# A two-layer hybrid trunk on one core: the attention heads' steps set further apart, and three output products taken together

## The chip, the cores and the metric

The kernel runs on one core of a Trainium2 chip. The metric is the time of one execution on the device in microseconds (us). All times are of one core; the profile shows one execution, taken by the hardware profiler.

The engines are called PE (TensorE, matrix products), ACT (ScalarE), DVE (VectorE), POOL (GpSimd) and SP (SyncE, which here issues the DMAs).

## The reference

A residual stream of 256 tokens by 2048 passes through two layers. In the first, the mixer is forgetting attention (FoX, 16 heads of 128); in the second, it is a dilated sliding-window attention (8 heads with values of 256; three groups of scores each). Every mixer stands behind an RMS norm and is followed by an RMS norm and a squared-ReLU MLP with 8192 hidden units. Everything is in 32-bit floating point.

```
def fox_attention(h, w_in, b_f, q_gain, k_gain, w_out):
    proj = h @ w_in
    q, k, v, f = jnp.split(proj, [H * dh, 2 * H * dh, 3 * H * dh], axis=-1)
    q = rms_norm(q.reshape(B, S, H, dh), q_gain)      # per head; k in the same way
    c = jnp.cumsum(jax.nn.log_sigmoid(f + b_f), axis=1)
    s = q @ k^T * dh**-0.5 + c[query] - c[key]         # causal
    o = softmax(s) @ v
    return o @ w_out

def dilated_attention(...):                            # q and k per group g, one shared v
    for g, (window, r) in enumerate(((128, 1), (512, 4), (2048, 16))):
        # causal window of 128 steps of stride r, ALiBi slope per (g, head)
    # the groups' numerators and denominators merged; o @ w_out

def reference(...):
    for i in range(2):
        x = x + mixer_i(rms_norm(x, mix_norm_g[i]))
        x = x + relu(rms_norm(x, mlp_norm_g[i]) @ w_up)**2 @ w_down
```

## The kernel before

**Products in three parts.** A 32-bit matrix product is made of three products of reduced-width operands: high part by high part, high by low, low by high. Each operand is therefore held as a cast high part and a low part, which is what the cast left over. Weights arrive from memory in chunks of 2048 rows by 512 columns, by DMAs of two tiles of 128 rows (`raw`). `split` (from L321) makes two such tiles ready at a time: a cast on ACT (`wh`, L333) and a subtraction on DVE (`wl`, L334). There are five buffers of `wh` and `wl`, so a cast must wait until PE has used up an older pair.

**Steps.** `product_steps` (L356) works through a chunk in 16 *steps*. One step is one 128-row tile of the weights against both halves of the 256 tokens: 6 products of 128 by 512 (L368 to L370). After each step the program calls `jobs.tick()`.

**The order of the work.** Everything that is not a product is a *job*: a Python generator that issues some instructions and then says `yield n`, which means that it goes on after n further steps, or `yield key`, which means that it goes on once the named result has been issued. So the program is interleaved while it is written down, by counting steps. From step 24 on, `pin()` fixes the order on each engine to that in which the instructions were written. No engine can go on with a later instruction when an earlier one waits. A wait behind `behind(...)` only puts an instruction behind another in that order.

**The jobs in the attention layers.** In FoX, the columns are worked in four groups `j` of four heads: a chunk of queries, one of keys, one of values. In the dilated layer, there are four groups `q4` of two heads.

* `qk_chain` (L543) norms a chunk of queries or keys: squares on ACT (`sq`), their sums on DVE (`ss`, L553 and L554), a power on POOL (L556), scaling on DVE (`rq`, `qn`, L560 and L562), a transpose of 32 by 32 blocks on DVE (L571), eight block moves to memory and two back over SP, and at last the casts on ACT (L595) and subtractions on DVE (L597).
* `fox_head` (L760) loads the bias, adds the mask (L773), and lets PE form the scores (`sc_f`, L687 and L690). DVE adds the bias and takes the maximum (`nm_f`, L789), ACT takes the exponential (L792), DVE scales by the denominator (L797).
* `p_turned` (L634) transposes the probabilities by way of memory: 32 by 32 blocks on DVE (L638), four block moves, one move back. `p_split` (L648) makes the high part on ACT (`pTh`, L653) and the low part on DVE (`pTl`, L655). Then `pv` (L618) forms the product with the values (`po_f`, `po_d`; L627 and L628) and splits its result into high (`oTfh`, L630) and low part (`oTfl`, L631), which the output product takes.
* `dil_head` (L810) does the same with three sets of scores (`sc_d`, added to the distances in `sd`, L823), one maximum (`nm_d`, L829) and one exponential (L832) for the three. The last of the eight heads is turned by PE (`p_transposed`, `ptp_d`, L662) and not by way of memory.

**Output products and norms.** `out_proj` (L901) multiplies the heads' results by the output weights, four chunks of 512 columns. `in_pair` (L382) takes the first two chunks together: the first 12 rows of one, the first 12 of the other, then the last 4 of each; so the last heads have 24 steps until their rows are wanted. `add_chain` (L878) adds the result to the residual stream and starts the next norm's transposition (`norm_chain`, L492). The tables of distances for the dilated layer (`dilation_tables`, L209) are made at the beginning of the first MLP.

## Time and profile before

| | |
|---|---|
| median of 3 runs | 2225.78 us (2223.76 to 2228.35) |
| profiled execution, its own time | 2224.2 us |
| its span in the profile | 2222.5 us |
| mean granted clock of PE | 0.99 |
| PE busy | 2161.3 us, 97% |
| weight loads of PE (PEld), beside it | 1915.4 us, 86% |
| DVE busy | 1431.6 us, 64% |
| ACT busy | 1089.2 us, 49% |
| DMA moved | 471.57 MB, 212 GB/s on average |

The span is what lies between the first and the last instruction; the execution's own time is 1.7 us longer. Busy times are sums over the whole span. A row of the wait view says which instruction waited for which, how long in total, how often, and the longest. A row of the window view gives the busy time of each engine in one stretch of time. Names of tiles stand without their numbers where rows are grouped. Lines (L655) are those of the kernel before.

### The profile page before, as it was taken

The page shows a single profiled execution, that of the slowest core. Times are in us where ns is not written, and L with a number is a line of the kernel's source. Part 1 is how long each engine was busy: PE and PEld are TensorE (multiplying, and loading weights), DVE is VectorE, ACT ScalarE, POOL GpSimd, SP SyncE. Part 2 cuts the span into 40 slices and gives each one's busy share as a digit, 9 for nine tenths or more (in the row PEclk, how much of TensorE's full clock was granted, in tenths as well). Part 3 has the DMA queues.
Part 4 walks back from the last instruction along what each step waited for, and adds up shares of the span by engine and source line. Part 5 has one row for each costly group of instructions (what it writes and reads, how often), then busy time and mean ns, then how long its engine had stood idle before and what let it go on. Part 6 is the DMA issues. An engine that isn't in the chain of part 4 may idle for free.

```text
span 2222.5 us, 29937 instructions
## 1 busy us (share of the span) xinstructions
PE 2161.3 (97%) x11123; PEld 1915.4 (86%) x11123; DVE 1431.6 (64%) x1892; ACT 1089.2 (49%) x1522; POOL 53.0 (2%) x40
## 2 busy tenths in 40 slices
PE   9989888999999999999999999999999999999998
PEld 7877777888898898898888888878988988988987
DVE  6666766775565565566667787767665665665664
ACT  5544544654354354355555655545544444444442
POOL 0000000000000000000010000100000000000000
PEclk9999999999999999999999999999999999999999
DMA  7776675766656656656777767757666666666663
GB/s 243 220 231 203 199 233 189 257 201 217 205 184 218 205 184 217 204 185 232 257 223 239 234 205 238 229 191 247 226 209 202 203 203 201 202 203 202 200 213 133
DMA packets 313810, 471.57 MB, mean 212 GB/s; under 512 B 35832, under 2 KB 123328, under 8 KB 313664
## 3 DMA queue, kind: packets, MB, share of 16 engines
q1 hardware_dynamic: 313072, 468.99, 65.8%
q8 instruction: 87, 1.43, 0.3%
q10 hardware_dynamic: 560, 0.66, 0.1%
q14 instruction: 59, 0.48, 0.1%
q0 software_dynamic: 32, 0.02, 0.0%
HBM read 446.15 MB, written 23.42 MB: 211 GB/s over the span
## 4 chain that ended last, share of the span: by engine, by line
PE 75%; DVE 3%; DMA 2%; ACT 2%; issue 1%; SPq 1%; POOL 0%; ACTq 0%; DVEq 0%; POOLq 0%
PE acc L369 15%; PE acc L368 15%; PE acc L370 15%; PE up_n3a_acc L432 5%; PE up_n1a_acc L432 5%; PE up_n3a_tp L432 3%; PE up_n3a_sc L432 3%; PE up_n3a_acc L436 3%; PE up_n1a_tp L432 2%; PE up_n1a_acc L436 2%; PE up_n1a_sc L432 2%; DMA raw<-in_dil_w_in_dram 2%; DVE wl L334 1%; PE up_n3a_tp L436 1%; PE up_n3a_sc L436 1%
## 5 line engine op out<-in xcount | busy, mean ns | idle before, releaser
L334 DVE TENSOR_TENSOR wl<-raw,wh 128x1024 fp32r<-128x1024 f32 (+1 forms) x801 | 968.3, 1220 | 639.5 <-ACT wh L333 632.5
L333 ACT CAST wh<-raw 128x1024 fp32r<-128x1024 f32 (+1 forms) x801 | 828.3, 1045 | 868.2 <-PE acc L370 572.2
L368 PE MATMUL acc<-wh,hT_n 128*128 128x512 f32 x896 | 346.3, 387 | 0.1
L369 PE MATMUL acc<-wl,hT_n 128*128 128x512 f32 x896 | 343.5, 383 | 0.1
L370 PE MATMUL acc<-wh,hT_n 128*128 128x512 f32 x896 | 342.6, 383 | 0.0
L368 PE MATMUL acc<-wh,aTh_n1a 128*128 128x512 f32 x512 | 194.0, 379 | 0.0
L369 PE MATMUL acc<-wl,aTh_n1a 128*128 128x512 f32 x512 | 194.0, 379 | 0.0
L370 PE MATMUL acc<-wh,aTl_n1a 128*128 128x512 f32 x512 | 194.0, 379 | 0.0
L370 PEld LDWEIGHTS acc<-wh,hT_n 128*128 128x128 f32 x896 | 171.5, 191 | 24.9
L368 PEld LDWEIGHTS acc<-wh,hT_n 128*128 128x128 f32 x896 | 172.0, 192 | 23.9 <-ACT wh L333 0.5
L369 PEld LDWEIGHTS acc<-wl,hT_n 128*128 128x128 f32 x896 | 171.8, 192 | 23.4 <-DVE wl L334 0.4
L368 PE MATMUL acc<-wh,aTh_n3a 128*128 128x512 f32 x480 | 181.9, 379 | 0.0
L369 PE MATMUL acc<-wl,aTh_n3a 128*128 128x512 f32 x480 | 181.9, 379 | 0.0
L370 PE MATMUL acc<-wh,aTl_n3a 128*128 128x512 f32 x480 | 181.9, 379 | 0.0
L432 PE MATMUL up_n1a_acc<-hT_n,wh 128*128 128x512 f32 x512 | 181.6, 382 | 0.0
L432 PE MATMUL up_n3a_acc<-hT_n,wh 128*128 128x512 f32 x512 | 181.6, 382 | 0.0
L436 PE MATMUL up_n1a_acc<-hT_n,wl 128*128 128x256 f32 x512 | 139.6, 273 | 0.0
L436 PE MATMUL up_n3a_acc<-hT_n,wl 128*128 128x256 f32 x512 | 139.6, 273 | 0.0
L369 PEld LDWEIGHTS acc<-wl,aTh_n1a 128*128 128x128 f32 x512 | 96.8, 189 | 13.7
L370 PEld LDWEIGHTS acc<-wh,aTl_n1a 128*128 128x128 f32 x512 | 96.8, 189 | 13.7
L368 PEld LDWEIGHTS acc<-wh,aTh_n1a 128*128 128x128 f32 x512 | 96.8, 189 | 13.7
L432 PEld LDWEIGHTS up_n3a_acc<-hT_n,wh 128*128 128x128 f32 x512 | 96.8, 189 | 13.5
(680 smaller groups left out, 3183.6 us busy)
## 6 DMA issues: line engine op xcount, KB each, us to landing
raw<-in_mlp_w_up_dram SPq DMA_DIRECT2D x256, 512.0 KB, 4.4
raw<-in_mlp_w_down_dram SPq DMA_DIRECT2D x256, 512.0 KB, 4.4
raw<-in_dil_w_in_dram SPq DMA_DIRECT2D x192, 256.0 KB, 4.4
raw<-in_fox_w_in_dram SPq DMA_DIRECT2D x95, 512.0 KB, 5.0
raw<-in_fox_w_out_dram SPq DMA_DIRECT2D x32, 512.0 KB, 3.8
raw<-in_dil_w_in_dram SPq DMA_DIRECT2D x32, 512.0 KB, 3.8
raw<-in_dil_w_out_dram SPq DMA_DIRECT2D x32, 512.0 KB, 5.2
blocks_n<-turned_n SPq DMA_DIRECT2D x96, 64.0 KB, 3.6
```

The source lines that it names most:

```text
L333: issued["cast"] = nc.scalar.copy(hi[:, part, :], raw[:, part, :])
L334: issued["cut"] = nc.vector.tensor_sub(lo[:, part, :], raw[:, part, :], hi[:, part, :].bitcast(F32))
L368: nc.tensor.matmul(acc[t], ah[:, tok], hi, start=first, stop=False)
L369: nc.tensor.matmul(acc[t], ah[:, tok], lo, start=False, stop=False)
L370: issued["product"] = nc.tensor.matmul(acc[t], al[:, tok], hi, start=False, stop=last)
L432: issued["product"] = nc.tensor.matmul(banks[b], hi[:, i, col], in_turn(tokens.rearrange("p x s -> p (x s)"), P // 2), start=first, stop=last)
L436: nc.tensor.matmul(banks[b][:, 0:S], lo[:, i, col], in_turn(tokens[:, 0, :], P // 2), start=False, stop=False)
```

## The change

Nothing is computed differently but for the turning of the last dilated head. What changes is the number of steps between the instructions of the jobs, and with it the order on every engine.

* **Scores to values.** In `fox_head` the exponential stands two steps behind the scores and not one, the scaling four and not two, the move back nine and not six, the high cast of the turned probabilities fifteen and not eleven, the low subtraction seventeen (two steps behind its cast and no longer with it), and the values nineteen and not thirteen or fourteen. In the last group (j = 3) the cast stands at fourteen, the subtraction at sixteen and the values at seventeen. The heads start at (3, 9, 21, 27) and, in the last group, (3, 8, 13, 17).
* **Bias.** It is loaded eight steps ahead of the scores, and added two steps ahead of them.
* **Dilated heads.** The three scores stand two steps apart, the exponential two steps behind the last, and the values as in FoX. The second head of a group starts eight steps behind the first. The last head of all is turned by way of memory like the others. Within `pv`, the low part of a head's result is subtracted a step behind the cast.
* **Query and key norms.** The casts on ACT stand three steps earlier, and the subtractions on DVE two steps behind their casts.
* **Output products.** Three chunks and not two are taken together, behind both attention layers; the third has its own banks (`ps_tp`). The norm of the third chunk starts after six steps and not two.
* **Tables and the rest.** `dilation_tables` waits for 40 steps and then issues a piece every four steps. The squares of the norm go to another buffer (`sd`). The low part of the values is subtracted a step later; the gate's `c_q` has two steps instead of one.

```diff
 def out_proj / add_out                       # the plan of loads follows the same order
-        if pair:
-            in_pair(lambda n: sums(), lambda acc, ks: product_steps(acc, keys, lhs, ks), posts)
-        for n in range(2 if pair else 0, NX):
+        if group:
+            in_group(lambda n: sums(*(() if n < 2 else (ps_tp, "tp"))),
+                     lambda acc, ks: product_steps(acc, keys, lhs, ks), posts[0:group])
+        for n in range(group, NX):
...
 def qk_chain
-        yield 7
-        for t in range(NT):
-            yield 2
+        yield 6
+        for t in range(NT):
+            subs = []
...
                 nc.scalar.copy(a, of)
-                with behind(issued["cut"]):
-                    nc.vector.tensor_sub(b, of, a.bitcast(F32))
+                subs.append((b, of, a))
+            yield 2
+            for b, of, a in subs:
+                nc.vector.tensor_sub(b, of, a.bitcast(F32))
...
 def pv
             nc.scalar.copy(hi, by_token(po))
+            yield 1
             nc.vector.tensor_sub(lo, by_token(po), hi.bitcast(F32))
...
 def p_turned / p_split
-        yield 4
+        yield 5
         move(turned.rearrange("p i b r -> p (i b r)"), blocks.rearrange("j c i x -> (j c) (i x)"))
-        yield 5
+        yield landing
...
         with behind(issued["cast"]):
             nc.scalar.copy(hi, first)
+        yield 2
         with behind(issued["cut"]):
             nc.vector.tensor_sub(lo, first, hi.bitcast(F32))
...
 def fox_head
-        at = ((2, 4, 6, 9) if j == 3 else (2, 8, 20, 26))[hh]
+        at = ((3, 8, 13, 17) if j == 3 else (3, 9, 21, 27))[hh]
...
-            yield at - 4
+            yield at - 8
...
-        yield 4
+        yield 6
         nc.vector.tensor_add(bias, bias, tables["mask"])
+        yield 2
...
-        turned = yield from p_turned(s, f"f{h}")
+        turned = yield from p_turned(s, f"f{h}", 5 if j == 3 else 6)
         yield ("fv", j)
-        pt_sb = p_split(turned, f"f{h}")
-        yield 2 if j == 3 else 3
+        pt_sb = yield from p_split(turned, f"f{h}")
+        yield 1 if j == 3 else 2
...
 def dil_head
-        yield (5 if q4 == 3 else 6) * i + 2
+        yield 8 * i + 3
...
-        if (q4, i) == (3, 1):
-            yield 2
-            pt_sb = p_transposed(p, f"d{h}")
-        else:
-            turned = yield from p_turned(p, f"d{h}")
-            yield ("dv", q4)
-            pt_sb = p_split(turned, f"d{h}")
-        yield 3
+        turned = yield from p_turned(p, f"d{h}", 6)
+        yield ("dv", q4)
+        pt_sb = yield from p_split(turned, f"d{h}")
+        yield 2
```

How this moves the instructions shows at three places on DVE. In the rows, the number behind a name is the tile's, `wl` is the low part of two tiles of weights, `ss`, `rq`, `qn` and `sq` belong to the norm of the next chunk of queries or keys, `pTl` is the low part of a head's turned probabilities and `oTfl` that of its result.

*First place: the third head of the first FoX group (`f2`), whose probabilities are finished while the keys of the second group are normed.* Before:

```order
L638 STREAM_TRANSPOSE turned_f3_1373<-s_f3_1343 128x3x4x32
L334 TENSOR_TENSOR wl44_1393<-raw44_1244,wh44_1392 128x1024
L553 TENSOR_REDUCE ss_('fk', 1)_1404<-sq_('fk', 1)_0_1400 128x4
L553 TENSOR_REDUCE ss_('fk', 1)_1404<-sq_('fk', 1)_1_1402 128x4
L554 TENSOR_SCALAR ss_('fk', 1)_1404<-ss_('fk', 1)_1404 128x8
L655 TENSOR_TENSOR pTl_f2_1419<-turned_f2_1291,pTh_f2_1418 128x256
L334 TENSOR_TENSOR wl45_1429<-raw45_1279,wh45_1428 128x1024
```

And of the change:

```order
L642 STREAM_TRANSPOSE turned_f3_1397<-s_f3_1335 128x3x4x32
L554 TENSOR_REDUCE ss_('fk', 1)_1408<-sq_('fk', 1)_0_1404 128x4
L554 TENSOR_REDUCE ss_('fk', 1)_1408<-sq_('fk', 1)_1_1406 128x4
L555 TENSOR_SCALAR ss_('fk', 1)_1408<-ss_('fk', 1)_1408 128x8
L600 TENSOR_TENSOR fqT1_0l_928<-sq_('fq', 1)_0_1144,fqT1_0h_927 128x256
L600 TENSOR_TENSOR fqT1_1l_931<-sq_('fq', 1)_0_1144,fqT1_1h_930 128x256
L335 TENSOR_TENSOR wl45_1433<-raw45_1274,wh45_1432 128x1024
L561 TENSOR_SCALAR rq_('fk', 1)_1412<-rq_('fk', 1)_1412,rstd_n0_111 128x4
L563 TENSOR_TENSOR qn_('fk', 1)_0_1445<-acc32_0_1154,rq_('fk', 1)_1412 128x512
...
L335 TENSOR_TENSOR wl46_1469<-raw46_1298,wh46_1468 128x1024
L335 TENSOR_TENSOR wl47_1491<-raw47_1328,wh47_1490 128x1024
L660 TENSOR_TENSOR pTl_f2_1481<-turned_f2_1303,pTh_f2_1480 128x256
```

The low part of the head's probabilities stood ahead of the norm's scaling, for which POOL has to be waited, and stands behind it now, with three weights between.

*Second place: the last heads of FoX.* Before:

```order
L631 TENSOR_TENSOR oTfl_12_3286<-po_f13_0_3317,oTfh_12_3285 128x256
L655 TENSOR_TENSOR pTl_f14_3325<-turned_f14_3185,pTh_f14_3324 128x256
L334 TENSOR_TENSOR wl110_3335<-raw110_3179,wh110_3334 128x1024
L631 TENSOR_TENSOR oTfl_14_3347<-po_f14_0_3348,oTfh_14_3346 128x256
L334 TENSOR_TENSOR wl111_3362<-raw111_3221,wh111_3361 128x1024
```

And of the change:

```order
L635 TENSOR_TENSOR oTfl_12_3311<-po_f13_0_3384,oTfh_12_3310 128x256
L335 TENSOR_TENSOR wl114_3405<-raw114_3255,wh114_3404 128x1024
L335 TENSOR_TENSOR wl115_3426<-raw115_3299,wh115_3425 128x1024
L660 TENSOR_TENSOR pTl_f14_3411<-turned_f14_3264,pTh_f14_3410 128x256
L335 TENSOR_TENSOR wl116_3453<-raw116_3328,wh116_3452 128x1024
L635 TENSOR_TENSOR oTfl_14_3439<-po_f14_0_3440,oTfh_14_3438 128x256
```

The head's low part stood ahead of the weights 110 and stands behind the weights 115 now.

*Third place: the first head of the second dilated group (`d2`), beside the second head (`d3`) and the norm of the next group.* Before:

```order
L838 TENSOR_TENSOR p_d3_11552<-p_d3_11552,sd3_11481 128x384
L638 STREAM_TRANSPOSE turned_d3_11557<-p_d3_11552 128x3x4x32
L334 TENSOR_TENSOR wl460_11571<-raw460_11415,wh460_11570 128x1024
L553 TENSOR_REDUCE ss_('dqk', 2, 0)_11581<-sq_('dqk', 2, 0)_0_11577 128x4
...
L554 TENSOR_SCALAR ss_('dqk', 2, 0)_11581<-ss_('dqk', 2, 0)_11581 128x8
L334 TENSOR_TENSOR wl461_11602<-raw461_11444,wh461_11601 128x1024
L655 TENSOR_TENSOR pTl_d2_11609<-turned_d2_11461,pTh_d2_11608 128x256
L560 TENSOR_SCALAR rq_('dqk', 2, 0)_11585<-rq_('dqk', 2, 0)_11585,rstd_n2_3885 128x4
```

And of the change:

```order
L824 TENSOR_REDUCE nm_d3_11557<-sd3_11500 128x1 x2
L554 TENSOR_REDUCE ss_('dqk', 2, 0)_11565<-sq_('dqk', 2, 0)_0_11561 128x4
...
L335 TENSOR_TENSOR wl461_11587<-raw461_11434,wh461_11586 128x1024
L561 TENSOR_SCALAR rq_('dqk', 2, 0)_11569<-rq_('dqk', 2, 0)_11569,rstd_n2_3869 128x4
...
L335 TENSOR_TENSOR wl462_11626<-raw462_11463,wh462_11625 128x1024
L830 RECIPROCAL den_d3_11558<-den_d3_11558 128x2
...
L642 STREAM_TRANSPOSE turned_d3_11638<-p_d3_11633 128x3x4x32
L335 TENSOR_TENSOR wl463_11658<-raw463_11484,wh463_11657 128x1024
L335 TENSOR_TENSOR wl464_11682<-raw464_11523,wh464_11681 128x1024
L660 TENSOR_TENSOR pTl_d2_11671<-turned_d2_11493,pTh_d2_11670 128x256
```

Here too the scaling of the norm, and besides it that of the second head, now stand ahead of the first head's low part.

More of the change, by code (lines that the diff above doesn't have):

```diff
@@ L241, in add, with add_group @@
             plan.append((w, r, cols))
-    def add_pair(*chunks):
+    def add_group(*chunks):
         for rows in ((0, CUT * P), (CUT * P, D)):
@@ L249, in add_out @@
     def add_out(w):
-        add_pair(*((w, [(n * NC, NC)]) for n in range(2)))
-        for n in range(2, NX):
+        add_group(*((w, [(n * NC, NC)]) for n in range(3)))
+        for n in range(3, NX):
             add(w, (0, D), [(n * NC, NC)])
@@ L261, in add_mlp @@
             if b == 0:
-                add_pair(*((mlp_w_up[l], [(n * NC, NC)]) for n in range(2)))
+                add_group(*((mlp_w_up[l], [(n * NC, NC)]) for n in range(2)))
             for n in range(0 if b else 2, 4):
@@ L272, in trunk @@
         if q4 == 0:
-            add_pair((dil_w_in[0], value), (dil_w_in[0], heads[0]))
+            add_group((dil_w_in[0], value), (dil_w_in[0], heads[0]))
         for cols in heads[1:] if q4 == 0 else heads + [value]:
@@ L353, in trunk, with sums @@
     used = [0]
-    def sums():
-        return [ps_acc.tile([P, NC], F32, tag="acc", name=f"acc{used[0]}_{t}") for t in range(NT)]
+    def sums(pool=ps_acc, tag="acc"):
+        return [pool.tile([P, NC], F32, tag=tag, name=f"acc{used[0]}_{t}") for t in range(NT)]
     def product_steps(acc, keys, lhs, steps):
@@ L380, in product, with in_group @@
         jobs.spawn(post(acc))
-    def in_pair(new, steps, posts):
+    def in_group(new, steps, posts):
         banks = []
-        for n in range(2):
+        for n in range(len(posts)):
             banks.append(new(n))
             steps(banks[n], range(CUT))
-        for n in range(2):
+        for n in range(len(posts)):
             steps(banks[n], range(CUT, KC))
@@ L656, in p_split @@
         return p_hi, p_lo, turned[:, :, 2, :]
-    def p_transposed(p, name):
-        pt = ps_tp.tile([P, 3 * P], F32, tag="tp", name=f"ptp_{name}")
-        for b in range(3):
-            nc.tensor.transpose(pt[:, b * P:(b + 1) * P], p[:, b * P:(b + 1) * P], ident)
-        p_hi, p_lo = (work.tile([P, S], F32R, tag=f"pT{x}", name=f"pT{x}_{name}", bufs=2) for x in "hl")
-        p_whole = work.tile([P, P], F32, tag="s", name=f"pTw_{name}", bufs=S_BUFS)
-        nc.scalar.copy(p_hi, pt[:, 0:S])
-        nc.vector.tensor_sub(p_lo, pt[:, 0:S], p_hi.bitcast(F32))
-        nc.scalar.copy(p_whole, pt[:, S:3 * P])
-        return p_hi, p_lo, p_whole
     def heads_pair(name, slot, keys):
@@ L953, in mlp @@
             if b == 0:
-                in_pair(lambda n: up_banks(key, n), steps, posts)
+                in_group(lambda n: up_banks(key, n), steps, posts[0:2])
             for n in range(0 if b else 2, 4):
```

44 lines of the change are left out of this document (23 added, 21 removed).

## The prediction

> **What bounds the kernel now.** I read the page first, then busy time by stage, then who keeps TensorE (PE) waiting.
>
> ```profile
> PE 2161.3 (97%) x11123; PEld 1915.4 (86%) x11123; DVE 1431.6 (64%) x1892; ACT 1089.2 (49%) x1522; POOL 53.0 (2%) x40
> ```
>
> PE is the bound: what can be gained is its idle time and its slow time. The windows below are the FoX layer with its projections, the first MLP, the dilated layer, the second MLP, and 50 us of undisturbed products (columns: window, length, busy time and instructions of PE, PEld, DVE, ACT, POOL, granted clock, DMA share, GB/s).
>
> ```profile
> 12.00:362.00 350.00, 311.41 (x1466) 267.36 (x1466) 242.38 (x432) 180.52 (x311) 17.41 (x11) 0.95 0.71 219
> 362.00:1205.00 843.00, 842.05 (x4403) 751.81 (x4402) 538.06 (x651) 413.80 (x550) 11.75 (x6) 1.00 0.67 216
> 1205.00:1485.00 280.00, 269.16 (x1301) 234.08 (x1300) 210.47 (x308) 155.39 (x231) 20.57 (x8) 0.98 0.70 223
> 1800.00:1850.00 50.00, 50.00 (x233) 43.80 (x232) 30.04 (x32) 22.29 (x26) 0.00 (x0) 1.00 0.61 203
> ```
>
> The last row gives the unit of time: 50.00/233 = 0.2146 us a product, six to a step (one 128-row of a weight chunk), so **1.29 us a step**. PE's idle time is 350.00−311.41 = 38.6 in FoX, 0.95 in the MLP and 10.8 in the dilated layer: **50.4 us**. Its causes:
>
> ```profile
> PE po_f L627 <- ACT pTh_f L653: 18.7, 5, 4.8
> PE po_f L627 <- DVE pTl_f L655: 14.0, 9, 2.3
> PE sc_d L687 <- DVE sd L823: 7.2, 8, 3.2
> PE sc_f L690 <- ACT fkT_0h L595: 3.4, 4, 1.5
> PE ptp_d L662 <- DVE p_d L840: 3.2, 1, 3.2
> PE sc_f L690 <- DVE fkT_0l L597: 1.4, 4, 0.4
> PE up_n1a_tp L436 <- DVE wl L334: 0.9, 1, 0.9
> ...
> ACT s_f L792 <- DVE nm_f L789: 78.1, 16, 9.5
> DVE bias L773 <- DMA bias<-negc: 33.5, 7, 6.4
> ACT wh L333 <- PE acc L370: 572.2, 369, 7.2
> ```
>
> (What waits, for what: total, times, longest.) Two thirds, 18.7+14.0, is the value product (po_f) standing for its turned probabilities (pTh, pTl). Behind that stand DVE, held up to 6.4 us by the bias landing, and ACT, held up to 9.5 by DVE's maximum: every engine runs its recorded order, so one late instruction holds the weights behind it. The last row sets the pace: ACT's weight casts wait for PE to give buffers back, so ACT and DVE cannot work ahead.
>
> A second loss is the clock. Seven stretches of half clock in the body sum to 44.38 us:
>
> ```profile
> sum 44.38, PE 31.74 PEld 25.60 DVE 35.89 ACT 20.00 POOL 6.82; mean PE 4.53 PEld 3.66 DVE 5.13 ACT 2.86 POOL 0.97
> ...
> 271.62:275.03 3.41, 0.84 (x4) 0.37 (x3) 3.34 (x8) 3.41 (x6) 0.00 (x0) 1.00 0.48 144
> 275.03:278.44 3.41, 3.41 (x11) 2.87 (x11) 3.38 (x6) 0.45 (x2) 1.04 (x1) 0.50 0.71 202
> 1206.87:1210.28 3.41, 1.42 (x9) 1.37 (x10) 3.41 (x6) 0.00 (x0) 0.00 (x0) 1.00 0.49 115
> 1210.28:1213.69 3.41, 3.41 (x10) 2.69 (x9) 1.91 (x4) 0.00 (x0) 0.00 (x0) 0.50 0.76 217
> ...
> 187.00:194.00 7.00, 5.05 (x24) 4.16 (x23) 5.16 (x12) 5.67 (x11) 0.00 (x0) 1.00 0.47 156
> ```
>
> 31.74 us of work at half clock would have taken half: **15.9 us** lost. The two pairs show the trigger: a 3.41 us stretch of which PE is idle 2.57 (and 1.99) is followed by one at 0.50, costing 3.41/2 = 1.7. The last row holds 1.95 us idle that straddled two such stretches, and the clock stayed 1.00. So a wait of about 2 to 3 us may or may not cost another 1.7.
>
> **The change part by part.** Scores to values grows from A+13 to A+19 (A: the step behind which the scores stand), the hi cast (pTh) at A+15, the lo subtraction (pTl) at A+17. Six steps are 7.7 us more, against the longest wait of 4.8: the ACT term (18.7) goes. The bias goes out 8 steps ahead of the scores and is added 6 steps after it leaves, 7.7 us against 5.2 before; its longest lateness was 6.4 beyond where DVE stood, but that also held later landings, so I take the 33.5 as gone. The dilated scores stand two steps apart instead of one, and the third's exponential two behind it: the 7.2 of sc_d goes. The three transposes of the last dilated head and their 3.2 go; MLP's 0.95 goes with the mask tables spread over its start.
>
> What is late next? pTl now stands on DVE two steps behind its cast, and in the order it has passed the query/key norm of the next group. This is DVE in the kernel before:
>
> ```profile
> 194.15 1.22 DVE L334 TENSOR_TENSOR wl<-raw,wh 128x1024 fp32r<-128x1024 f32 x1
> 195.28 0.68 DVE L553 TENSOR_REDUCE ss_('fq', 2)_1847<-sq_('fq', 2)_0_1843 128x4 f32<-128x512 f32 x1
> ...
> 196.58 0.17 DVE L554 TENSOR_SCALAR ss_('fq', 2)_1847<-ss_('fq', 2)_1847 128x8 f32<-128x8 f32 x1
> ...
> 199.42 0.23 DVE L560 TENSOR_SCALAR rq_('fq', 2)_1851<-rq_('fq', 2)_1851,rstd_n 128x4 f32<-128x4 f32 x1 [1.19 <-POOL rq_('fq', 2)_1851 L556]
> ...
> 202.37 1.18 DVE L334 TENSOR_TENSOR wl<-raw,wh 128x1024 fp32r<-128x1024 f32 x1
> 203.47 0.41 DVE L655 TENSOR_TENSOR pTl_f<-turned_f,pTh_f 128x256 fp32r<-128x256 f32 x1
> 203.81 1.22 DVE L334 TENSOR_TENSOR wl<-raw,wh 128x1024 fp32r<-128x1024 f32 x1
> 204.94 0.55 DVE L773 TENSOR_TENSOR bias<-bias,mask 128x384 f32<-128x384 f32 x1
> ```
>
> Prices, start to start: a weight remainder (wl) 195.28−194.15 = 1.13, about 1.2 with its wait for ACT; the sums of squares (ss) 1.3; from their end (196.75) over POOL's power to rq 2.67; the rq, qn and transposes up to the next wl 202.37−199.42 = 2.95; pTl 0.34 to 0.4. A wl whose cast has just been released is finished 2.4 later (cast 1.05 + wl 1.2, rows of the page's groups, and the handing over).
>
> *Third head of groups 0 to 2* (f2, f6, f10). Count from the end of step A+10, when PE gives a buffer back. wl ends at 2.4, or at 3.6 where ACT first does the exponential and the four query casts, 146.66−144.97 = 1.7 by these rows:
>
> ```profile
> 144.97 0.51 ACT L588 ACTIVATE sq_('fq', 1)_0_1147<-qn_('fq', 1)_1_1198,gain 128x256 f32<-128x256 f32 x1
> ...
> 146.66 1.04 ACT L333 CAST wh<-raw 128x1024 fp32r<-128x1024 f32 x1
> ```
>
> I take 3.6. The fourth head's scaling and transpose take 1.3 (4.9), ss 1.3 (6.2), two query subtractions 0.7 (6.9); POOL from ss's end holds rq until 8.85; the block ends 11.8, two wl 14.1, pTl 14.5. It is wanted behind step A+19, 9×1.29+0.1 = 11.75: late by **2.75**, by 1.7 if ACT is not held. I take 2.6, three times: 7.8.
>
> *First head* (f0, f4, f8). From the end of A+12: wl 2.4, ss 3.7, POOL to 6.4, block 9.35, wl 10.5, bias add 11.0, pTl 11.4. Wanted at 7×1.29 plus a score group of PE, 119.16−118.60 = 0.56 below, plus 0.1, so 9.7: late **1.7**, three times: 5.1. Second and fourth heads have no norm ahead of pTl: about 0.
>
> ```profile
> 118.60 0.38 PE L687 MATMUL sc_f<-fkT_1w,fqT_1w 128*128 128x128 f32 x2
> ...
> 119.16 0.38 PE L368 MATMUL acc<-wh,hT_n 128*128 128x512 f32 x1
> ```
>
> *Last four FoX heads.* Their values stand one step behind pTl (2 in the other groups). f12, f14 and f15 have pTl behind a wl released by the same step: 2.4+0.4 = 2.8 against 1.4, late 1.4 to 1.85; f13's comes ahead. Together **4.8**.
>
> *Dilated groups 0 to 2.*
>
> ```profile
> 1216.58 0.17 DVE L835 RECIPROCAL den_d<-den_d 128x2 f32<-128x2 f32 x1 [0.30 <-ACT sd L832]
> ...
> 1218.92 1.18 DVE L334 TENSOR_TENSOR wl<-raw,wh 128x1024 fp32r<-128x1024 f32 x1
> ...
> 1223.07 1.42 DVE L829 TENSOR_REDUCE nm_d<-sd 128x1 f32<-128x384 f32 x2
> ```
>
> The head's scaling group is 1218.92−1216.58 = 2.34, its maximum 1.42. First head, from the end of A+12: wl 2.4, the other head's score 0.5 and maximum (4.3), ss 5.6, POOL 8.25, block 11.2, wl 12.35, scaling group 14.7, two wl 17.0, pTl 17.4; wanted at 11×1.29+0.55+0.1 = 14.85: late **2.55**. Second head, pTl behind ss: 0.9. Three times 3.45: 10.35. The last group has no norm behind it: 0.
>
> *Rest.* The last row of the dilated output products needs a remainder written two steps before it and behind a wl: 1.2. The first scores of a group keep part of fkT's 3.4+1.4, because ACT's key casts stand two steps earlier and in order: 0.6 × 3 = 1.8.
>
> Left idle: 7.8+5.1+4.8+10.35+1.2+1.8 = **31.0 us**. Each is below 2.8, so some will fall whole into one 3.41 us stretch: of twelve waits of 1.4 to 2.8 I take four, **7 us** (none to eight: 0 to 14).
>
> *Edits at nothing.* Output products in threes: 36 steps (46 us) instead of 24 stand before the first late row, so nothing waits for a head there; the third product's banks are free until the MLP. Its longer way to the next norm (6 steps) is covered by the 24 product steps of the last two chunks; uncovered it would be 5 us. Tables and squares (junk): DVE has 20 of each 50 us free (the 1800 row). DMAs: bias and block moves change steps on SP's queue, ahead of weight loads:
>
> ```profile
> raw<-in_fox_w_in_dram SPq DMA_DIRECT2D x95, 512.0 KB, 5.0
> ```
>
> A load lands 5.0 after its issue; PE's buffers hold eight steps, 10.3 us, of cast weights, so I count nothing, and bound it by rival 3.
>
> The three transposes save a little beside the wait ahead of them:
>
> ```profile
> L662 PE MATMUL ptp_d<-ident,p_d x3: 421/469/477, 1480.9 to 1481.4; 128*128 128x128 f32 x3
> ```
>
> From the first start to the last end (1481.4+0.47) that is 0.9 to 1.0; I take 0.9.
>
> **The sum**, against the profiled execution: 2224.2 − 50.4 − 15.9 − 0.9 + 31.0 + 7 = 2195.0. That execution is 1.6 below the median 2225.78: about **2197**.
>
> **Rivals.**
> 1. *The cover is complete.* DVE takes up its lateness between heads, as in the MLP, where it is busy 30 of 50: only the last four heads and the tail wait. 2224.2 − 67.2 + 6 + 1.6 = about 2165. For it: six steps are 7.7 us, more than any wait on record. Against: buffers keep DVE from working ahead (the 572.2), so the 2.67 for POOL comes inside the path each time. Chance 0.15.
> 2. *The clock stays whole.* All waits left are below 2.8; if only stretches that are idle throughout lowered it, the 7 would be 0: 2197 − 7 = about 2190. For: the 187 row. Against: 2.57 idle in the 271.62 row, followed by 0.50. The Trainium skill ("TensorE: Matmul & The Clock Gate", section "HAM oscillation — how this bites in real kernels") states the abstract rule as "no PE-idle gaps >~3.4µs"; by it no wait left here would cost clock. The trace disagrees: the 2.57 us were enough. Chance 0.12.
> 3. *Slower: the norm's landings hold ACT.* The query/key casts now stand on ACT three steps earlier behind the move that brings the norm back, and ahead of weight casts. If the move lands later than that, ACT stands, no weights follow and PE starves at each of the 15 norms (of 20) that run beside heads. The move's longest landing:
>
> ```profile
> qn_('fk', 3)_1_2845<-blocks_('fk', 3)_1_2854 SPq DMA_DIRECT2D x1, 256.0 KB, 5.6
> ```
>
> Six steps, 7.7 us, are left for it, so it is late only where its issue is: behind the eight block moves, which wait for DVE's transposes and so for POOL's 2.67. Price: 2197 + 15 × lateness; it decides from 1.9 us each (28.8/15); with POOL's whole 2.67 uncovered, 2237. Against: DVE needs to be late by 2.1 + 1.9 before that. Chance 0.08.
> 4. *The waits only move.* Work that leaves the head delays the next head's scores by as much, and the two losses stay 66 us: 2224.2 − 0.9 + 1.6 = about 2225. For: pTl has passed a whole norm in the order. Against: the ACT wait that carried 18.7 has six steps more. Chance 0.07.
>
> **How the numbers follow.** The forecast case has 0.58: about 2197, in itself 2180 to 2214 (the 31 a third less or more, the clock 0 to 14). A measurement of this kernel can tell about 0.2% (4.5 us). Faster: forecast, 1 and 2, 0.85; within: 0.07; slower: 0.08. The range, down to rival 1 and short of rivals 3 and 4, is 2162 to 2212.
>
> **What would show it.** Right: among PE's waits po_f for pTh is gone and po_f for pTl is about 18 us at nine heads, po_d for pTl about 10; no DVE wait for bias, no ptp_d; POOL ahead of each late pTl on DVE; about four half-clock stretches. Wrong: po waits under 6 us (rival 1), no stretch at 0.50 (rival 2), ACT waiting for DMA at the query/key casts with PE behind wl (rival 3), idle time of PE still near 50 (rival 4).

## The result and the profile after

The changed kernel takes 2206.84 us (median of 6 runs, 2205.34 to 2210.05) against 2224.04 us before (6 runs): a ratio of 0.9923, with a 95% interval of 0.9910 to 0.9936. It is 17 us faster. The forecast was 2197 us, with a range of 2162 to 2212. The profiled execution took 2206.94 us.

The page's first part after the change:

```profile
PE 2152.4 (98%) x11120; PEld 1911.1 (87%) x11120; DVE 1423.7 (65%) x1893; ACT 1095.2 (50%) x1521; POOL 45.9 (2%) x40
```

Busy time by stage, in windows that fit both kernels (FoX, the first MLP, the dilated layer with its output product). Before:

```profile
12.00:370.00 358.00, 319.41 (x1504) 274.35 (x1504) 246.13 (x437) 183.84 (x317) 17.41 (x11) 0.95 0.71 220
...
1150.00:1500.00 350.00, 339.16 (x1636) 295.62 (x1635) 256.19 (x368) 195.67 (x289) 28.38 (x11) 0.99 0.71 225
```

After:

```profile
12.00:370.00 358.00, 338.36 (x1652) 293.48 (x1652) 261.55 (x456) 200.06 (x330) 18.08 (x9) 1.00 0.77 237
370.00:1150.00 780.00, 780.00 (x4110) 697.77 (x4109) 494.36 (x597) 381.78 (x510) 6.10 (x6) 1.00 0.67 214
1150.00:1500.00 350.00, 326.81 (x1565) 285.30 (x1564) 242.18 (x353) 186.35 (x270) 18.43 (x10) 0.97 0.68 214
```

The two layers went opposite ways. In FoX, PE is busy 19 us more of the same 358 (338.36 against 319.41), and its clock is whole. In the dilated layer it is busy 12 us less of 350 (326.81 against 339.16). What PE waits for after the change:

```profile
PE po_f L630 <- DVE pTl_f L660: 15.7, 11, 1.8
PE po_d L630 <- DVE pTl_d L660: 13.3, 6, 3.3
PE sc_d L680 <- DVE sd L817: 7.9, 1, 7.9
PE sc_f L683 <- DVE fkT_0l L600: 2.7, 1, 2.7
...
PE acc L371 <- DVE oTdl L635: 1.0, 1, 1.0
PE acc L370 <- DVE wl L335: 0.8, 1, 0.8
PE pct L746 <- DVE c_q L742: 0.8, 1, 0.8
PE pf L694 <- DVE wfs L193: 0.2, 1, 0.2
```

The waits for pTh, 18.7 us before, are gone, as are those of the transposes; the waits for pTl are there as forecast. The third line is not: a single wait of 7.9 us for the scores of a dilated head. The rows sum to 42.4 us, where 31.0 had been forecast and 50.4 had been there before. (The rows left out stand at the very beginning and end and are the same in both kernels to 0.1 us.)

What stands behind the 7.9 shows in ACT's waits for the move that brings a norm back. In the kernel before there is no such wait among these casts; after, the first dilated group has three, each longer than the last:

```profile
ACT dqT_2w L589 <- DMA qn_('dqk', 0, 2)_0_10474<-ks_('dqk', 0, 2)_0_10480: 10.4, 1, 10.4
...
ACT dqT_1w L589 <- DMA qn_('dqk', 0, 1)_0_10259<-ks_('dqk', 0, 1)_0_10265: 6.7, 1, 6.7
ACT fkT_0w L589 <- DMA qn_('fk', 0)_0_770<-blocks_('fk', 0)_0_776: 4.9, 1, 4.9
...
ACT dqT_0w L589 <- DMA qn_('dqk', 0, 0)_0_10065<-ks_('dqk', 0, 0)_0_10071: 3.2, 1, 3.2
```

The row of 4.9 belongs to the first key norm of FoX and stands ahead of the 2.7 us that PE waits for the first scores (`sc_f`).

The longest, 10.4, in the timelines of SP, ACT, DVE and PE (start, length, instruction, and in brackets the idle time before it):

```profile
1159.85 2.84 SPq L291 DMA_DIRECT2D ks_('dqk', 0, 2)_1_10486<-sq_('dqk', 0, 2)_1_10415  x4
...
1164.77 0.47 SPq L291 DMA_DIRECT2D qn_('dqk', 0, 2)_0_10474<-ks_('dqk', 0, 2)_0_10480  x1
...
1170.39 0.51 ACT L589 ACTIVATE dqT_2w<-qn_('dqk', 0, 2)_0_10474,gain 128x256 f32<-128x256 f32 x1 [10.45 <-DMA qn_('dqk', 0, 2)_0_10474<-ks_('dqk', 0, 2)_0_10480]
...
1172.82 1.23 DVE L335 TENSOR_TENSOR wl<-raw,wh 128x1024 fp32r<-128x1024 f32 x1 [8.64 <-ACT wh L334]
...
1176.70 0.68 DVE L554 TENSOR_REDUCE ss_('dqk', 1, 0)_10632<-sq_('dqk', 1, 0)_0_10628 128x4 f32<-128x512 f32 x1
...
1184.09 0.54 DVE L817 SCALAR_TENSOR_TENSOR sd<-dist,sc_d 128x384 f32<-128x384 f32 x1
...
1184.68 0.58 PE L680 MATMUL sc_d<-dkT_2w,dqT_2w 128*128 128x128 f32 x1 [7.94 <-DVE sd L817]
```

The move back goes out at 1164.77, behind four weight loads and the block moves that wait for DVE's transposes, and lands at 1170.4, 5.6 us later. ACT stands for it in its order, with the weight casts behind it; so the next norm's squares come late, its transposes with them, and the next move back lands later still. DVE has nothing to subtract while ACT stands (8.64 us). What PE waits for at 1184.68 is not weights, for which it stood only 0.8 us, at 1159.69. It is room for scores: there are two banks for them, and the third set has to wait until DVE's addition of the first (`sd`) has freed one. In DVE's order that addition stands behind the late weights and behind the whole norm of the next group, from the sums at 1176.70 on, and comes at 1184.09. In the kernel before, PE waited 3.2 us at the same place, without any of these landings.

Half clock after the change, first the stretch behind that wait, then the sum of five stretches, four in the body and one near the end:

```profile
1179.83:1190.07 10.24, 5.39 (x15) 4.57 (x16) 9.29 (x15) 0.63 (x1) 0.17 (x1) 0.50 0.63 182
...
sum 23.88, PE 19.03 PEld 15.88 DVE 16.71 ACT 3.78 POOL 1.46; mean PE 3.81 PEld 3.18 DVE 3.34 ACT 0.76 POOL 0.29
```

19.03/2 = 9.5 us are lost. Of these, 1.7 lie near the end, behind a wait of 2.2 us that the kernel before has too, there without a drop of the clock. The body loses 7.8, where 7 had been forecast and 15.9 were lost before.

### The profile page after: what moved, and what is told of

It is laid out like the page before. It is cut to its first block, busy times and chain, and to the rows that moved or that the text cites. A ratio compares the mean times of both kernels' runs of the same rounds, so it can differ in the third digit from the quotient of the medians.

```text
span 2205.2 us, 29959 instructions
## 1 busy us (share of the span) xinstructions
PE 2152.4 (98%) x11120; PEld 1911.1 (87%) x11120; DVE 1423.7 (65%) x1893; ACT 1095.2 (50%) x1521; POOL 45.9 (2%) x40
## 4 chain that ended last, share of the span: by engine, by line
PE 83%; DVE 6%; DMA 5%; ACT 2%; issue 2%; SPq 1%; POOL 1%; ACTq 0%; DVEq 0%; POOLq 0%
PE acc L369 16%; PE acc L371 16%; PE acc L370 16%; PE up_n1a_acc L433 5%; PE up_n3a_acc L433 5%; DVE wl L335 3%; DMA raw<-in_dil_w_in_dram 3%; PE up_n1a_sc L433 3%; PE up_n3a_sc L433 3%; PE up_n1a_tp L433 3%; PE up_n3a_tp L433 3%; PE up_n3a_acc L437 3%; PE up_n1a_acc L437 3%; ACT wh L334 2%; PE up_n3a_tp L437 1%
```

## The experiments

All ratios are to the kernel before, run on the same chip beside the experiment. Where several kernels are compared with each other, this is by their medians; the kernel before measured 2223.1 to 2224.2 us beside the several experiments, so such differences are good to about a us.

### Later casts, later values, and both

Three kernels take the changed kernel and move the norm's casts three steps later, or the values two steps later, or both. First, the casts:

```diff
-        yield 6
+        yield 6 if key == ("dqk", 3, 2) else 9
         for t in range(NT):
             subs = []
```

> The changed kernel with the query/key casts three steps later behind their move back (nine steps and not six, but for the last norm of the dilated layer), and with them the subtractions, the heads and all behind them; distances within a head unchanged. Theory 1 (the early casts hold ACT for the landing, and POOL with the norm's block of DVE stands ahead of pTl): the 7.94 us wait of sc_d, most of the 2.7 of sc_f and the half clock at 1180 go (about -13), and since the norm's block now stands five to seven steps ahead of pTl of the first and third FoX heads and not two to four, their six waits of 1.7 fall to about 0.2 each; the second dilated heads get the block one step ahead of pTl and wait about 3.5 each. Together about 2176 us. Rival (the engines are simply too full around the heads, wherever the norm stands): the waits move along with the heads, 2200 to 2207.

Measured: 2196.57 us, ratio 0.9880 (0.9865 to 0.9894). The waits of sc_d are gone, that of sc_f fell to 0.3, and of ACT's stands of 3.2, 6.7 and 10.4 us for the moves of the first dilated group this is left:

```profile
ACT dqT_2w L589 <- DMA qn_('dqk', 0, 2)_0_10472<-ks_('dqk', 0, 2)_0_10478: 0.2, 1, 0.2
```

The first and third heads of FoX groups 0 to 2 had waited 1.7 us each; five of these six now wait for nothing, one 0.4. But the fourth heads, which had waited for nothing in two groups and 0.6 us in one, now wait 1.8 to 2.2, the dilated heads wait somewhat longer for pTl in all (14.8 against 13.3), and the first of them for pTh too:

```profile
PE po_d L630 <- DVE pTl_d L660: 14.8, 6, 2.8
PE po_f L630 <- DVE pTl_f L660: 9.1, 9, 2.2
PE po_d L630 <- ACT pTh_d L657: 3.4, 3, 1.4
```

So the cause of the 7.9 is shown to be the place of the casts and of the heads behind them; the edit moves the two together and does not part them. (Weights are split at every second step, and three is odd, so the edit also moves the heads from a step with weights to one without; what that can weigh comes up below.) The size of the gain was wrong, 2176 us against 2196.57, since new waits took the place of the old. SP's timeline at a first dilated head shows it:

```profile
1194.68 1.86 SPq L291 DMA_DIRECT2D ks_('dqk', 1, 1)_1_10930<-sq_('dqk', 1, 1)_1_10862  x4
...
1197.14 0.41 SPq L291 DMA_DIRECT2D turned_d<-pblocks_d  x1
```

With the heads three steps later, the head's own move back stands on SP behind the eight block moves of the norm.

Then the values:

```diff
-        yield 1 if j == 3 else 2          # FoX, between pTl and the values
+        yield 1 if j == 3 else 4
...
-        yield 2                           # dilated
+        yield 2 if q4 == 3 else 4
```

> The changed kernel with the values two steps later (A+21) in FoX groups 0 to 2 and dilated groups 0 to 2; the rest as it is. Theory 1: the waits for pTl are fixed latenesses of 1.7 to 3.3 us, so 2.58 us more takes them nearly all away (29 us to about 6, four of them in the last FoX group), and about 5 us of half clock with them; the 7.94 wait of sc_d stays, since it comes from the early casts: about 2179 us. Rival (the lateness is not fixed, DVE falls behind without end beside the heads): waits stay about as long, 2200 or more. Second rival (7.94 is due to the values' place): it goes as well, about 2168.

Measured: 2196.52 us, ratio 0.9877 (0.9862 to 0.9892). The sc_d wait stays at 7.9, as expected of a cause that lies in the casts. Of the 29 us for pTl, 19 are left (9.6 and 9.5), not 6, and the time is 2196.52 and not 2179: the first heads' waits are gone in groups 0 to 2, but where a head's move lands late, ACT holds the weights and the next group's keys, and the first scores of the four groups wait 7.4 us in all (2.7 after the change). ACT at the fourth head of the first group:

```profile
152.47 0.40 ACT L657 CAST pTh_f<-turned_f 128x256 fp32r<-128x256 f32 x1 [4.34 <-DMA turned_f<-pblocks_f]
```

Both:

> Both edits together: casts three steps later and values two steps later. Theory 1: the two add up, since they take away different waits: PE idle in the body about 7 us and one half-clock stretch at most, about 2163 us. Rival: they overlap or the values now stand against the next group's work, 2175 or more.

Measured: 2170.44 us, ratio 0.9762 (0.9747 to 0.9776). Each edit alone gains 10 us on the changed kernel, both together 36. They do not merely add up, they help each other: the wait that the later casts opened at the values is what the later values cover. The 2163 that had been expected were missed by 7.

### The group of three

```diff
-        add_group(*((w, [(n * NC, NC)]) for n in range(3)))     # and the products with it
+        add_group(*((w, [(n * NC, NC)]) for n in range(2)))
```

> The changed kernel with the output products in pairs again (24 steps and not 36 before the first late row; waits of the norms as before). By the order, PE has nothing to do for 9 steps at the end of FoX and for 12 at the end of the dilated layer, until the last heads' values stand. Theory: the group of three is what the six steps more of a head are paid with: 15 to 27 us of PE idle time more and two to four us of half clock, about 2227 us, so the whole gain is gone. Rival (the last heads are ready long before, the counted steps only set the order): 2207 to 2212.

Measured: 2217.50 us, ratio 0.9978 (0.9968 to 0.9987), 10.7 us over the changed kernel. The theory holds in kind; the size lay below the range. PE's waits sum to 49.5 us and not 42.4, so 7 more and not 15 to 27. I take it that steps without products, as counted, are not idle time: once no products are issued, the head's chain runs at its own speed. No run tests this.

The same group alone in the kernel before:

```diff
-            in_pair(lambda n: sums(), lambda acc, ks: product_steps(acc, keys, lhs, ks), posts)
+            in_pair(lambda n: sums(*(() if n < 2 else (ps_tp, "tp"))), ..., posts[0:3])
```

> The kernel before with the three output products taken together alone (and the third norm's longer way), heads, norms and tables as before. Theory: the group is not a gain by itself, it only makes room for later values: within 3 us of before, about 2222 to 2227. Rival (the last heads were late for the first late rows in the kernel before, so the group alone gains): 2214 or less.

Measured: 2226.26 us, ratio 1.0015 (1.0005 to 1.0025). The group gains nothing by itself; it makes room.

### POOL's power

```diff
         nc.gpsimd.tensor_tensor(rq, ss, ..., ALU.pow)
-        yield 3
+        yield 3 if key == ("dqk", 3, 2) else 6
```

> The changed kernel with six steps and not three between POOL's power and DVE's scaling of the norm (but for the last norm), everything behind it three steps later, the casts six steps behind their move as in the change. So DVE no longer stands for POOL (1.5 us in the trace after), and the norm's block is issued two and four steps ahead of pTl of the first and third FoX heads, one step after pTl of the second dilated head. Counting DVE's order with the durations of the trace: first FoX heads late by about 2.1, third 0.2, first dilated 1.1, second 0.2; PE waits for pTl about 11 us and not 29. The casts' move is issued when its blocks are there, so the landing holds ACT less and the 7.9 of sc_d falls to 0 to 4. About 2180 us. Rival (what stands in order ahead of pTl does not matter, only how many steps a head has): 29 us stay, about 2200.

Measured: 2198.28 us, ratio 0.9887 (0.9872 to 0.9902). The waits for pTl are 21.9 us (10.7 and 11.2) and not 11, sc_d's 5.5 and not 0 to 4. As a time this is the rival's 2200; the waits lie between theory and rival (29 us). The count along DVE's order was off by up to 1.3 us at the first and third FoX heads (1.4 each against 2.1; 1.5, 0.7 and 0.2 against 0.2) and by up to 3.1 at the second dilated heads (1.8, 2.9 and 3.3 against 0.2), and that is the size of the waits themselves. That POOL holds DVE at the first FoX heads and not at the third shows in the changed kernel itself. DVE ahead of the first head's pTl:

```profile
112.04 1.23 DVE L335 TENSOR_TENSOR wl<-raw,wh 128x1024 fp32r<-128x1024 f32 x1
114.79 0.23 DVE L561 TENSOR_SCALAR rq_('fq', 1)_1152<-rq_('fq', 1)_1152,rstd_n 128x4 f32<-128x4 f32 x1 [1.53 <-POOL rq_('fq', 1)_1152 L557]
...
119.32 0.42 DVE L660 TENSOR_TENSOR pTl_f<-turned_f,pTh_f 128x256 fp32r<-128x256 f32 x1
```

and of the third's:

```profile
139.26 0.17 DVE L555 TENSOR_SCALAR ss_('fk', 1)_1408<-ss_('fk', 1)_1408 128x8 f32<-128x8 f32 x1
...
141.29 0.23 DVE L561 TENSOR_SCALAR rq_('fk', 1)_1412<-rq_('fk', 1)_1412,rstd_n 128x4 f32<-128x4 f32 x1
...
146.48 0.42 DVE L660 TENSOR_TENSOR pTl_f<-turned_f,pTh_f 128x256 fp32r<-128x256 f32 x1
```

At the first head DVE stands 1.53 us for POOL; at the third, rq comes 1.9 us behind the sums' end and DVE stands for nothing. The power itself takes longer at the query norm than at the key norm; why, no run shows:

```profile
112.14 2.62 POOL L557 TENSOR_TENSOR rq_('fq', 1)_1152<-ss_('fq', 1)_1148,mhalf 128x8 f32<-128x8 f32 x1 [43.31 <-DVE ss_('fq', 1)_1148 L555]
139.51 1.74 POOL L557 TENSOR_TENSOR rq_('fk', 1)_1412<-ss_('fk', 1)_1408,mhalf 128x8 f32<-128x8 f32 x1 [24.75 <-DVE ss_('fk', 1)_1408 L555]
```

In the dilated layer DVE stands 1.5 us for POOL at the first norms of groups 2 and 3, ahead of the first heads of groups 1 and 2.

### The bias

```diff
-            yield at - 8
+            yield max(at - 4, 0)
...
-        yield 6
+        yield 4
         nc.vector.tensor_add(bias, bias, tables["mask"])
-        yield 2
```

> The changed kernel with the bias loaded four steps ahead of the scores and added right ahead of them (for the first head of a group as soon as it has landed by the steps), as in the kernel before, all else as in the change. Theory: DVE stands for the landing again, some 25 to 33 us in all as before, with weights and pTl behind it; at heads where PE already waits for pTl this adds 1 to 2 us each, 5 to 12 us in all: about 2212 to 2219. Rival (DVE's idle time covers it, as DVE has two fifths of its time free): within 3 us of 2207.

Measured: 2215.07 us, ratio 0.9967 (0.9955 to 0.9979), 8.2 us over the changed kernel. DVE stands 15.2 us for the bias (4.1 with the change; 25 to 33 had been expected), and po_f waits 19.9 us and not 15.7. The early bias is worth about 8 us.

### Which part of the change gained what

Heads as before, all else as in the change:

```diff
 pv, p_turned, p_split, p_transposed, fox_head, dil_head      # word for word as in the kernel before
```

> The changed kernel with the heads (scores, probabilities, values, bias) as in the kernel before, all other parts of the change in place. Theory: the heads' spacing carries more than the whole gain, and the early casts cost about 11: waits for pTh and pTl of some 33 us come back, about 2228 to 2236 us, slower than before. Rival (the gain lies in the norms, tables and products, not in the heads): 2215 or less.

Measured: 2226.32 us, ratio 1.0015 (1.0005 to 1.0024). The time lies just under what the theory gave, but the waits don't fit: those for pTh and pTl are 18.3 us and not 33, and 24.6 us are waits of dilated scores (sc_d). FoX and dilated layer of this run:

```profile
12.00:370.00 358.00, 340.76 (x1626) 294.96 (x1625) 257.85 (x450) 197.60 (x328) 15.17 (x9) 0.97 0.76 234
1150.00:1500.00 350.00, 318.29 (x1496) 276.39 (x1495) 232.92 (x346) 181.49 (x270) 16.80 (x10) 0.96 0.66 205
```

FoX is as busy as with the change (340.76 against 338.36) without any of the added steps, at a clock of 0.97 and not 1.00: the first product of the first MLP stands at 398.5 us, at 393.2 with the change and at 425.0 in the kernel before. What is lost against the change lies for the most part in the dilated layer. So FoX's gain can be had without the spacing. To divide it, the norms' casts were put back in the dilated layer alone:

```diff
+        late = key[0] == "dqk"
-        yield 6
+        yield 9 if late else 6
...                                      # late: each subtraction right behind its cast, as before
```

> Heads as in the kernel before in both layers (thirteen steps), group of three and tables as in the change, and the casts and subtractions of the norms as in the change in FoX but as before in the dilated layer. Theory: the run with all heads as before lost in the dilated layer what it had gained in FoX, and both lie in the norms' casts: FoX keeps about 17 us of PE idle time (before: 38), the dilated layer comes back to about 11 (32 in that run), with 6 to 9 us less of half clock: about 2196 us, faster than the changed kernel without any of its six steps. Rival (the dilated waits of that run come from the old heads themselves, or FoX's gain from elsewhere): 2215 or more.

Measured: 2196.32 us, ratio 0.9885 (0.9869 to 0.9902). Heads at thirteen or fourteen steps, and 10 us faster than the changed kernel:

```profile
12.00:370.00 358.00, 338.94 (x1627) 293.46 (x1627) 257.16 (x450) 197.84 (x328) 15.18 (x9) 0.98 0.75 234
1150.00:1500.00 350.00, 339.55 (x1659) 296.65 (x1658) 259.42 (x369) 192.91 (x281) 24.82 (x10) 1.00 0.71 224
```

In both layers PE is now about as busy as in the better of the two kernels, in FoX at a clock of 0.98. The time came as expected, but for FoX the reason given, the norms' casts, was still to be tested. What of the norm's edit helps there? It ends one step earlier, so every head that waits for it stands one step earlier. One more run puts that one step back:

```diff
-        at = ((2, 4, 6, 9) if j == 3 else (2, 8, 20, 26))[hh]
+        at = ((3, 5, 7, 10) if j == 3 else (3, 9, 21, 27))[hh]
...
-            yield 2                      # the first head, behind the keys
+            yield 3
```

> The run by layer (heads as in the kernel before, early casts in FoX alone) with every FoX head started one step later, which is the very step at which it stood in the kernel before. Weights are cast and subtracted at every second step; in the kernel before and here the scores stand behind a step with weights, in the run by layer behind one without. Theory 1 (what gained in FoX was that parity: DVE's maximum no longer stands behind a weight subtraction whose cast is just released, so ACT's exponential and the weights behind it are not held): the waits come back to 30 us or more in FoX, about 2212 to 2220 us. Theory 2 (what gained were the casts on ACT three steps earlier and the subtractions two steps behind them): within 5 us of 2196.

Measured: 2221.35 us, ratio 0.9989 (0.9980 to 0.9999). One step, in FoX alone, costs 25 us, and all that FoX had gained is gone:

```profile
12.00:370.00 358.00, 319.94 (x1501) 275.54 (x1501) 245.40 (x437) 185.18 (x316) 17.93 (x9) 0.94 0.71 220
```

ACT's waits for the maximum, first of the run by layer, then of this one:

```profile
ACT s_f L800 <- DVE nm_f L797: 30.5, 12, 4.6
```

```profile
ACT s_f L800 <- DVE nm_f L797: 75.6, 16, 9.3
```

The kernel before has 78.1, 16, 9.5. With the scores behind a step that also casts weights, DVE's maximum stands behind a weight subtraction, and ACT's exponential, one step on, holds the next weight cast; behind a step without weights it doesn't. The place is shown by the run; that this is how it acts is read from the two rows and the order, and was not tried apart. Nor does a run move the heads by two steps, which would part the kind of step from the place.

The same run also says what the spacing does in the changed kernel. There, the heads of FoX groups 0 to 2 start at the very steps of this run, with the same early casts and the same group of three. With nineteen steps and the early bias PE is busy 338.36 us of that window, with thirteen or fourteen and the late bias 319.94, and ACT's row for the maximum after the change is

```profile
ACT s_f L786 <- DVE nm_f L783: 0.4, 2, 0.2
```

So at this place the heads' edits do carry FoX's whole gain, the early bias about 8 us of it. The run with all heads as before did not show it, since its heads also stood one step earlier. There are two ways to the same gain: more room, or another step.

### A version that beats both

Reading the run with both edits, three places were changed: the values of the fourth FoX head of a group kept their old place, those of the third and of all dilated heads of groups 0 to 2 got three steps and not two, and the last FoX group's pTl stands one step behind its cast. The values' part of it, against the run with both:

```diff
-        yield 1 if j == 3 else 4
+        yield 2 if j == 3 else (4, 4, 5, 2)[hh]
...
-        yield 2 if q4 == 3 else 4
+        yield 2 if q4 == 3 else 5
```

> Casts three steps later and values later as in the run with both, with three differences read from that run's trace: the fourth head of FoX groups 0 to 2 keeps its old place (there the next group's values on ACT had to wait for PE, and the first scores then waited 2.3 us for what stands behind on DVE), the third head and all dilated heads of groups 0 to 2 get three steps more and not two, and in the last FoX group pTl stands one step behind its cast and the values two behind that. Theory (each wait is one lateness of known size): body idle 17.7 to about 6, both half-clock stretches gone: about 2156 us. Rival (later values only move the waits): 2168 to 2173.

Measured: 2174.95 us, ratio 0.9784 (0.9769 to 0.9799): 4.5 us slower than with both. The reading of the fourth head was wrong. In the run with both, ACT had stood 3.95 us for that head's move and only 0.2 for PE ahead of the waiting scores; now the values wait for the move themselves. SP and ACT:

```profile
291.24 0.50 SPq L291 DMA_DIRECT2D turned_f<-pblocks_f  x1
...
299.88 0.40 ACT L657 CAST pTh_f<-turned_f 128x256 fp32r<-128x256 f32 x1 [6.46 <-DMA turned_f<-pblocks_f]
```

Issued behind the norm's ten moves, it lands 8.6 us later. So the fourth head was started three steps earlier:

```diff
-        at = ((3, 8, 13, 17) if j == 3 else (3, 9, 21, 27))[hh]
+        at = ((3, 8, 13, 17) if j == 3 else (3, 9, 21, 24))[hh]
...
-        yield 2 if j == 3 else (4, 4, 5, 2)[hh]
+        yield 2 if j == 3 else (4, 4, 5, 3)[hh]
```

> The tuned run with the fourth head of FoX groups 0 to 2 started three steps after the third and not six, its values one step later relative to its scores, so that its move back on SP is issued ahead of the norm's two moves back and of two weight loads, and its values still stand ahead of the next group's. Theory: the waits for pTh and pTl at that head (14.2 us of the tuned run, and 6.6 of half clock) come from that move landing 8.6 us after a late issue; they go: about 2157 us. Rival (DVE and ACT cannot carry two heads so close together): 2168 or more.

Measured: 2166.64 us, ratio 0.9748 (0.9733 to 0.9762), the fastest of all, by 57 us against the kernel before and by 40 against the changed one. What is left for PE:

```profile
PE po_f L630 <- DVE pTl_f L660: 8.1, 5, 2.2
...
PE po_d L630 <- DVE pTl_d L660: 1.9, 3, 1.0
```

It missed its 2157 by 10: at the fourth head ACT still waits up to 7.0 us for the move, and 2.2 of that reach PE, three times, with two stretches at half clock behind them (6.5 + 3.4 = 9.9).

## Why the prediction was right or wrong

**The direction and the way held.** PE was the bound, the change took waits away from it, and what came in their place were waits for pTl on DVE. The ACT term (18.7) went, as did the transposes and the MLP's 0.95. Two of the signs named for it came out otherwise: DVE still stands 4.1 us for one bias, and POOL holds DVE ahead of the first heads' pTl, not of the third's. About 17 us came where 27 to 29 had been forecast.

**The terms of what is left**, forecast against measured (the single waits are PE's in the trace after):

| term | forecast | measured |
|---|---|---|
| first FoX heads, three | 5.1 | 5.3 (1.77 each) |
| third FoX heads, three | 7.8 (1.7 each if ACT is not held) | 5.1 (1.71 each) |
| last four FoX heads | 4.8 | 4.7 |
| dilated groups 0 to 2 | 10.35 | 13.3 |
| output product's last row | 1.2 | 1.0 |
| first scores | 1.8 | 2.7 |
| scores of a dilated head, and weights ahead of it | none | 8.7 |
| half clock in the body | 7 | 7.8 |

In all, 42.4 + 7.8 us are left where 31.0 + 7 had been forecast, 12.2 more; the profiled execution's 2206.94 lies 11.9 above the sum's 2195.0.

At the third heads the lower of the two values came out, but not by the path given for it, that ACT is not held: at the third head of the first group ACT does the exponential and the four query casts (131.93 to 134.50) ahead of the weight cast, as in the higher count. What was too large is POOL's 2.67. It is taken from a query norm, and the third heads stand behind a key norm, whose power takes 1.74 us (1.75 in the trace before), so that rq starts 1.9 behind the sums. That it came to the 1.7 written there is luck; by its own terms the working gives 14.5 − 1.2 − 11.75 = 1.55 there. In the dilated layer, the second heads (1.93, 3.33 and 1.31) were late by more than the 0.9 that was counted, the first (1.67, 2.56, 2.55) as counted at two of three. The first scores' 2.7 is not the 0.6 at each of three groups that was counted, but one wait at the first group, behind ACT's 4.9 us for a landing.

**The step that failed** is the zero for the casts that moved ahead, with rival 3 as its bound. The mechanism of that rival is what happened, in the dilated layer at one place and not at all fifteen norms: it was priced as lateness times the number of norms, with nothing in between. The trace shows two things that the price lacked. PE's cast weights can take up a lateness of some us whole, so single ones cost nothing in the dilated layer (ACT stands 4.2, 2.4 and 2.0 us at single norms of the last two groups, and PE's waits name neither weights nor scores behind them). And where three norms follow each other, each starts from the last one's lateness, 3.2, 6.7, 10.4, until DVE, with late weights and the next norm ahead of it in its order, adds the first scores so late that PE stands 7.9 us for their bank. The forecast had also counted the 7.2 of sc_d as gone by the two steps between the scores. With its clock, that place cost 7.9 + 0.8 + 2.7 = 11.4 us, more than the whole distance of 10 us between forecast and result. The run with later casts shows the cause, casts and heads moved together.

**Right for a reason that was not the only one:** "Six steps are 7.7 us more, against the longest wait of 4.8: the ACT term (18.7) goes." It did go, and in the changed kernel the room did it: from the same steps, heads with thirteen or fourteen steps lose all of FoX's gain (319.94 busy against 338.36). But two runs show that FoX did not need it: moved by one step, heads of thirteen or fourteen steps lose nearly as little (338.94, at a clock of 0.98). I had read ACT's 78.1 us for the maximum and DVE's 33.5 for the bias as lateness that only room could absorb; the one step takes ACT's waits from 75.6 to 30.5, the room takes them to 0.4. In the dilated layer PE is busy 318.29 us with the old heads and 326.81 with the new ones, both with early casts, against 339 before; there the old heads also stand one step earlier, so the early casts and the step are not parted.

**A slip in the count.** "Scores to values grows from A+13 to A+19": in FoX groups 0 to 2 the values stood at A+14, and in the last group they go from A+13 to A+17, so the heads get five steps more and four, not six. Five steps are 6.45 us, still above the 4.8, and the conclusion stands. For the dilated heads, six is right (17 to 23, counted from the first scores).

**The zeros that held:** the group of three by itself (1.0015). Without it the longer heads cost 10.7 us; it was no gain but the condition of one. The bias was worth 8 us, where I had counted its 33.5 on DVE as gone without a price of its own.

**Rivals.** Rival 1 (2165) needed the norms' casts and the values later and the fourth head elsewhere: the best run, 2166.64, is about that. Rival 2 fell: four stretches at half clock in the body and one near the end. Rival 4 did not come about as a whole, though the dilated layer is a case of it.

## What to carry to other kernels

Where every engine runs a fixed order, a job is not late by its own length but by what stands ahead of it in the order, and a shift by one step can weigh as much as five more steps of room. A wait that buffers hide is not free: look whether the next instance starts from its lateness, for then the sum is not of waits but of their growth. And two edits that each open a wait for the other should be tried together before either is judged.

## What the runs showed of the hardware

PE's clock is set in stretches of 3.41 us (within the fourteen profiles half clock lasts 3.41, 6.83 or 10.24 us, where the end does not cut it off), and the measure is how much of a stretch PE was idle. Two pairs of neighbouring stretches of the changed kernel:

```profile
1289.06:1292.47 3.41, 1.83 (x10) 1.69 (x11) 2.66 (x4) 0.38 (x1) 0.00 (x0) 1.00 0.79 233
1292.47:1295.88 3.41, 3.41 (x20) 3.04 (x19) 1.56 (x2) 1.42 (x2) 0.00 (x0) 1.00 0.93 267
1227.62:1231.03 3.41, 1.49 (x9) 1.14 (x9) 3.38 (x8) 1.68 (x3) 1.41 (x1) 1.00 0.52 161
1231.03:1234.44 3.41, 3.41 (x9) 2.70 (x9) 3.34 (x7) 1.04 (x1) 0.27 (x1) 0.50 0.46 152
```

Idle for 1.58 us, the next stretch is at full clock; idle for 1.92, the next is at half. Counted over the profiles of all fourteen kernels, behind the first 12 us, for stretches at full clock with 0.9 us or more idle: up to 1.7 us, 0 of 117 were followed by half clock; from 1.7 to 2.0 us, 7 of 21; above 2.0, all 76. So the limit lies at a little over half of a stretch, and a wait of 2 us costs 1.7 more (half of 3.41, at full work) or nothing, by where it falls. The Trainium skill ("TensorE: Matmul & The Clock Gate", section "HAM oscillation — how this bites in real kernels") gives the abstract rule as no idle gaps above about 3.4 us; these runs disagree, since gaps of 2 us inside one stretch were enough.
